# Moving the state decay, one gated C and the first state's matmul of each pair of scan chunks to earlier visits

## The chip, the core and the metric

The kernel runs on one NeuronCore of a Trainium2 chip. TensorE (PE) does matrix products into PSUM, VectorE (DVE), ScalarE (ACT) and GpSimd (POOL) work on elements, SyncE (SP) issues most of the transfers. Each engine takes its own instructions in order and waits on semaphores for the others. The metric is the device time of one execution in microseconds (us); for a version it is the median of its runs.

## The reference

One decoder layer for 1024 positions of width 1024. After a norm, one wide projection gives the inputs of two branches: a Mamba-2 scan (SSD) and forgetting attention; both are gated, merged, projected and added to x. The change touches the scan alone. Cut to that:

```python
# 16 heads of 64 channels in 4 groups that share B and C (state size 128); chunks of q = 128
da_cs = jnp.cumsum((dt * a).reshape(bsz, nc, q, g, r), axis=2)
decay = jnp.exp(jnp.where(causal[None, None, :, :, None, None], seg, -jnp.inf))
cb = jnp.einsum('bclgn,bcsgn->bclsg', cc, bc)
y_diag = jnp.einsum('bclsgr,bcsgrp->bclgrp', cb[..., None] * decay, xdt)
to_end = jnp.exp(da_cs[:, :, -1:] - da_cs)
states = jnp.einsum('bcsgn,bcsgrp->bcgrpn', bc, xdt * to_end[..., None])
chunk_decay = jnp.exp(da_cs[:, :, -1])
def step(carry, inp):
    st, dec = inp
    return carry * dec[..., None, None] + st, carry
_, prev = lax.scan(step, init, (jnp.moveaxis(states, 1, 0), jnp.moveaxis(chunk_decay, 1, 0)))
y_off = jnp.einsum('bclgn,bcgrpn->bclgrp', cc, prev) * jnp.exp(da_cs)[..., None]
y = (y_diag + y_off).reshape(bsz, seqlen, n_heads, p)
```

So a chunk's output is a part within the chunk (`y_diag`) and a part carried in by the state of the chunks before it (`y_off`), and the state goes from chunk to chunk: times the chunk's decay, plus the chunk's own contribution.

## The kernel before

All large projections run as one long stream of half products on PE (`Stream`, `Pair`; a half product is 6 matmuls of 128x128 by 128x512, a product is two of them). The weights are split into a high and a low part by ACT (line 350) and DVE (line 351) up to three products ahead into four `wop` buffers, and sums of weights come from line 356. Other work is woven in by generators: a generator does a piece of its work and yields a number n, and the stream then runs n half products (`beside`). Such a piece of work is called a visit here.

The scan is one such generator, `ssd(g)`, once for each of the four groups g of four heads. It goes over the 8 chunks in pairs (a, b = a + 1), so there are 16 pairs in the kernel. Per pair it makes these visits:

- the *turning visit*: `first(a)` and `first(b)` (line 845). PE transposes x and B and forms B^T C (tile `tr`); DVE forms `xdt` (x times dt, line 856), the masked B^T C (`cbm`, line 861) and the weighted decay matrix `m` (line 866); ACT copies the turned B (`bn`, line 864). Then `more(a)`, `more(b)` (line 881): on POOL `xe`, which is xdt times the decay to the chunk's end (line 888), on ACT the exponential of the summed decay in place in `csb` (line 894), on POOL its product with C, the gated C (line 895). The first chunk has no gated C, the last no `xe`.
- four half products, then the *output visit*: `state(a)` with the state matmul (tile `st`, one PSUM buffer), the decay multiply of the previous state on POOL (line 909) and the add on DVE (line 914; for chunk 0 a copy, line 906); `within(a)` (yps<-m,xdt), `carried(a)` (yps<-csb,new), `within(b)`, `carried(b)`, which reads the state that `state(a)` has just made; `state(b)`, whose state the next pair reads; `skipped` (line 944); and the loads of later rows of summed decays (`sums`, `csb`, three buffers).
- two half products, `decays(a + 2)` on ACT (lines 875 and 879: the decay matrix of a coming chunk), two more, `decays(b + 2)`, and the next turning visit.

The order on each engine: matmuls and everything wrapped in `pin` keep the order in which the program issues them. The rest may be set elsewhere in its engine's queue by the planner, which works with estimated times; `tc.high_priority()` puts an instruction further ahead. On POOL nearly everything in this stage is pinned, and besides the scan its queue holds the weight differences of the output projection (`weights_work`, tile `wd`, line 211), one now and then, each waiting for its own transfer.

Of the kernel before, what the change touches and what calls it, by code (L numbers as in the profile page):

```python
# [8 lines left out]
F32 = mybir.dt.float32  # L9
# [7 lines left out]
P = 128  # L17
# [4 lines left out]
NT = T // P  # L22
# [64 lines left out]
def hybrid_layer(ctx: ExitStack, tc, a, out):  # L87

    nc = tc.nc
# [37 lines left out]
    def mm(*args, **kw):  # L127
        return tc.keep_in_program_order(nc.tensor.matmul(*args, **kw))  # L128
# [679 lines left out]
    def turn_values():  # L808

        if turning and turning[0][0] + 2 <= stream.count:  # L810
            turning.pop(0)[1]()
# [22 lines left out]
    def ssd(g):  # L834
        xs, bt, ct = [groups[g][f"xs{j}"] for j in range(2)], groups[g]["bt"], groups[g]["ct"]
        hs = slice(4 * g, 4 * g + 4)
        at = [{} for _ in range(NT)]

        def sums(c):

            if c < NT:
                csb = at[c]["csb"] = sp.tile([P, 4, P], F32, tag="csb", bufs=3, name="csb")
                nc.sync.dma_start(csb, cs_dram[hs, c * P : (c + 1) * P].unsqueeze(0).to_broadcast([P, 4, P]))

        def first(c):

            cs = slice(c * P, (c + 1) * P)
            s = at[c]
            tr = pp.tile([P, HALF], F32, tag="tr", bufs=2, name="tr")
            turn(tr[:, 0:P], xs[0][:, cs])  # L850
            turn(tr[:, P : 2 * P], xs[1][:, cs])
            if c < NT - 1:
                turn(tr[:, 2 * P : 3 * P], bt[:, cs])
            mm(tr[:, 3 * P :], bt[:, cs], ct[:, cs], start=True, stop=True)
            xdt = s["xdt"] = sp.tile([P, 4, 64], F32, tag="xdt", bufs=2, name="xdt")
            nc.vector.tensor_tensor(  # L856
                xdt, tr[:, 0 : 2 * P].rearrange("p (h d) -> p h d", h=4),
                dtn[:, c, hs].unsqueeze(2).to_broadcast([P, 4, 64]), ALU.mult,
            )
            cbm = sp.tile([P, P], F32, tag="cbm", bufs=1, name="cbm")  # L860
            nc.vector.tensor_tensor(cbm, tr[:, 3 * P :], tri, ALU.mult)
            if c < NT - 1:
                bn = s["bn"] = sp.tile([P, P], F32, tag="bn", bufs=2, name="bn")
                nc.scalar.activation(bn, tr[:, 2 * P : 3 * P], AF.Copy)
            m4 = s["m4"]
            nc.vector.tensor_tensor(m4, m4, cbm.unsqueeze(1).to_broadcast([P, 4, P]), ALU.mult)

        def decays(c):

            if c < NT:  # L870
                csb = at[c]["csb"]
                m4 = at[c]["m4"] = sp.tile([P, 4, P], F32, tag="m4", bufs=2, name="m4")
                for h in range(4):
                    pin(
                        nc.scalar.activation(  # L875
                            m4[:, h, :], csb[:, h, :], AF.Relu, scale=-1.0, bias=cscol[:, c, 4 * g + h : 4 * g + h + 1]
                        )
                    )
                pin(nc.scalar.activation(m4, m4, AF.Exp, scale=-1.0))

        def more(c):

            cs = slice(c * P, (c + 1) * P)
            s = at[c]
            if c < NT - 1:
                xe = s["xe"] = sp.tile([P, 4, 64], F32, tag="xe", bufs=2, name="xe")
                pin(
                    nc.gpsimd.tensor_tensor(  # L888
                        xe, s["xdt"], tend[:, c, hs].unsqueeze(2).to_broadcast([P, 4, 64]), ALU.mult
                    )  # L890
                )
            if c > 0:
                ce = s["ce"] = s["csb"]
                pin(nc.scalar.activation(ce, ce, AF.Exp))
                pin(nc.gpsimd.tensor_tensor(ce, ce, ct[:, cs].unsqueeze(1).to_broadcast([P, 4, P]), ALU.mult))

        def state(c, prev):

            if c == NT - 1:
                return None  # L900
            s = at[c]
            st = pp.tile([P, 4, 64], F32, tag="st", bufs=1, name="st")
            mm(st, s["bn"], s["xe"], start=True, stop=True)
            new = sp.tile([P, 4, 64], F32, tag="prev", bufs=3, name="new")
            if c == 0:
                nc.vector.tensor_copy(new, st)
            else:
                pin(
                    nc.gpsimd.tensor_tensor(
                        new, prev, cdec[:, c, hs].unsqueeze(2).to_broadcast([P, 4, 64]), ALU.mult  # L910
                    )
                )
                with tc.high_priority():
                    nc.vector.tensor_tensor(new, new, st, ALU.add)
            return new

        def within(c, yps):
            s = at[c]
            cc = slice((c % 2) * P, (c % 2 + 1) * P)
            for j in range(2):  # L920
                for e in range(2):
                    h = 2 * j + e
                    mm(
                        yps[e * 64 : e * 64 + 64, j, cc], s["xdt"][:, h, :], s["m4"][:, h, :],
                        start=(c % 2 == 0 and j == 0), stop=(c == 0), skip_group_check=True,
                    )

        def carried(c, prev, yps):
            s = at[c]
            cc = slice((c % 2) * P, (c % 2 + 1) * P)  # L930
            for j in range(2):
                for e in range(2):
                    h = 2 * j + e
                    mm(
                        yps[e * 64 : e * 64 + 64, j, cc], prev[:, h, :], s["ce"][:, h, :], start=False, stop=True,
                        skip_group_check=True,
                    )

        def skipped(c, yps):

            c2 = slice((c - 1) * P, (c + 1) * P)
            for j in range(2):
                i = 2 * g + j
                nc.vector.scalar_tensor_tensor(
                    xs[j][:, c2], xs[j][:, c2], dsk[:, i : i + 1], yps[:, j, :], ALU.mult, ALU.add
                )

        prev = early = None
        for c in range(3):
            sums(c)  # L950
        yield 2
        decays(0)
        yield 2
        decays(1)
        for a in range(0, NT, 2):
            b = a + 1
            with tc.high_priority():
                first(a)
                first(b)
            if early:  # L960
                next(early, None)
            more(a)
            more(b)
            yield 2
            turn_values()
            yield 2
            yps = pp.tile([P, 2, 2 * P], F32, tag="y", bufs=1, name="yps")
            mid = state(a, prev)
            within(a, yps)
            if a:  # L970
                carried(a, prev, yps)
            within(b, yps)
            carried(b, mid, yps)
            prev = state(b, mid)
            skipped(b, yps)
            sums(a + 3)
            sums(a + 4)
            if early:
                next(early, None)
            if a == 2:  # L980

                z = sp.tile([P, T + 4], F32, tag="u", bufs=2, name="z")
                early = squares(g, 0, [z[:, half(j)] for j in range(2)])
                next(early)
            turn_values()
            yield 2
            decays(a + 2)
            turn_values()
            yield 2
            decays(b + 2)  # L990
        if g == NG - 1:
            while turning:
                turning.pop(0)[1]()
                yield 1
# [89 lines left out]
    def gated(i):  # L1084

        y, g = {}, {}

        def begin(ch):
            g[ch] = small()
            nc.sync.dma_start(g[ch], gs_dram[i, :, half(ch)])  # L1090

        begin.early = True

        def dst(ch):
            y[ch] = small()
            return y[ch]

        def post(ch):
            stream.after(1, lambda: times(y[ch], g[ch], ch))

        def times(y, g, ch):
            nc.vector.scalar_tensor_tensor(y, g, 1.0, y, ALU.add, ALU.mult)
            pin(nc.gpsimd.dma_start(ms_dram[i, :, half(ch)], y))

        return dst, post, begin
# [85 lines left out]
    ends = [final("wbs", i, gated, ops_s, nc.vector) for i in range(4)]  # L1191
# [4 lines left out]
    with tc.tile_pool(name="pro", bufs=1, reuse_waits="tile", side="right") as pro, tc.tile_pool(  # L1196
        name="prop", bufs=1, space=PSUM, reuse_waits="tile", side="right"
# [11 lines left out]
        early = ExitStack()  # L1209
# [142 lines left out]
    with tc.tile_pool(name="att", bufs=1, reuse_waits="tile", side="right") as ap, tc.tile_pool(  # L1352
# [237 lines left out]
        state, deferred = {}, []  # L1590
# [227 lines left out]
```

## Time and profile before

| | |
|---|---|
| time, median of 3 runs | 1312.7 us (1307.1 to 1314.98) |
| the profiled execution | 1316.44 us, its span 1314.7 us |
| mean granted TensorE clock | 0.986 of full speed |
| PE idle in the span | 1314.7 - 1259.9 = 54.8 us |
| scan stages | four, between about 127 and 656 us of the span |

How to read the lines that follow: in the table of busy times an engine's time stands with its share of the span. In the list of waits a line names the engine, the tile it was to write, and whom it waited for, then the total, the number of waits and the longest. A row by window gives the window, its length, the busy time of PE, PE's weight loads, DVE, ACT and POOL with the number of instructions, the granted clock, the share of the DMA engines and GB/s. A row of the timeline gives start, length, engine, line, operation and tiles (out<-in), and in brackets how long the engine had sat idle before it and who ended that. A row by tile gives the shortest, median and longest duration in ns, and the first and last start.

### The profile page before, as it was taken

The page shows a single profiled execution, that of the slowest core. Times are in us where ns is not written, and L with a number is a line of the kernel's source. Part 1 is how long each engine was busy: PE and PEld are TensorE (multiplying, and loading weights), DVE is VectorE, ACT ScalarE, POOL GpSimd, SP SyncE. Part 2 cuts the span into 40 slices and gives each one's busy share as a digit, 9 for nine tenths or more (in the row PEclk, how much of TensorE's full clock was granted, in tenths as well). Part 3 has the DMA queues.
Part 4 walks back from the last instruction along what each step waited for, and adds up shares of the span by engine and source line. Part 5 has one row for each costly group of instructions (what it writes and reads, how often), then busy time and mean ns, then how long its engine had stood idle before and what let it go on. Part 6 is the DMA issues. An engine that isn't in the chain of part 4 may idle for free.

```text
span 1314.7 us, 20757 instructions
## 1 busy us (share of the span) xinstructions
PE 1259.9 (96%) x6928; PEld 997.1 (76%) x6928; DVE 1022.4 (78%) x1993; ACT 787.4 (60%) x1719; POOL 320.4 (24%) x321
## 2 busy tenths in 40 slices
PE   6999889998999989998999999999999999999998
PEld 4688678887877878886788777777776777778886
DVE  7989866987678967897777766777689777797975
ACT  7746555556555655565554666666687666753754
POOL 3000421004310232003400223233112212347152
PEclk9999989999999989999999999999999999999999
DMA  8232533545335434454337556666688666756933
GB/s 292 79 118 69 157 106 109 179 158 184 100 118 195 136 106 145 151 164 159 120 126 257 171 193 211 218 220 202 214 268 283 230 209 217 256 177 226 365 114 103
DMA packets 152235, 233.56 MB, mean 178 GB/s; under 512 B 15200, under 2 KB 60736, under 8 KB 152128
## 3 DMA queue, kind: packets, MB, share of 16 engines
q1 hardware_dynamic: 136064, 196.08, 46.3%
q10 hardware_dynamic: 10560, 18.06, 3.6%
q0 software_dynamic: 5504, 18.09, 3.6%
q8 instruction: 54, 0.88, 0.3%
q14 instruction: 53, 0.43, 0.1%
HBM read 162.99 MB, written 72.34 MB: 179 GB/s over the span
## 4 chain that ended last, share of the span: by engine, by line
PE 40%; DVE 5%; DMA 5%; ACT 3%; issue 2%; POOL 1%; SPq 0%; DVEq 0%; ACTq 0%; POOLq 0%
PE pb L128 15%; PE pc L128 10%; PE av L128 4%; PE s L128 4%; PE pt L131 4%; PE pd L128 2%; DVE wop L351 1%; DMA xr<-in_x 1%; DMA x3l<-t_s 1%; ACT ex L1534 1%; DMA raw<-in_wbs 1%; DMA x4l<-t_w 1%; ACT wop L350 0%; DMA th<-gs_dram 0%; ACT m L875 0%
## 5 line engine op out<-in xcount | busy, mean ns | idle before, releaser
L350 ACT ACTIVATE wop<-sum 128x512 fp32r<-128x512 f32 x180 | 112.4, 627 | 126.3 <-DVE sum L356 47.0
L351 DVE TENSOR_TENSOR wop<-sum,wop 128x512 fp32r<-128x512 f32 x180 | 144.4, 803 | 48.9 <-ACT wop L350 48.0
L1534 ACT ACTIVATE ex<-ex,nm 128x512 f32<-128x512 f32 (+1 forms) x192 | 116.2, 606 | 74.8 <-DVE nm L1530 74.3
L410 ACT ACTIVATE s<-pb 128x512 f32<-128x512 f32 x143 | 84.7, 593 | 92.7 <-PE pb L128 90.7
L351 DVE TENSOR_TENSOR wop<-raw,wop 128x512 fp32r<-128x512 f32 x144 | 106.6, 741 | 33.3 <-ACT wop L350 33.1
L128 PE MATMUL pb<-x5h,wop 128*128 128x512 f32 x376 | 132.0, 409 | 0.5 <-ACT s L410 0.5
L128 PE MATMUL pb<-x0h,wop 128*128 128x512 f32 x384 | 132.3, 401 | 0.0
L128 PE MATMUL pb<-x4h,wop 128*128 128x512 f32 x384 | 130.5, 399 | 1.5 <-ACT wop L350 1.1
L128 PE MATMUL pc<-x3h,wop 128*128 128x512 f32 x384 | 130.5, 397 | 0.4 <-DVE ot L427 0.4
L128 PE MATMUL pc<-x2h,wop 128*128 128x512 f32 x384 | 129.8, 396 | 0.0
L128 PE MATMUL pb<-x6h,wop 128*128 128x512 f32 x376 | 127.4, 397 | 1.3 <-ACT s L410 1.3
L1530 DVE CUSTOM_DVE_ANT_0 ex<-s,fb 128x512 f32<-128x512 f32 (+1 forms) x192 | 96.8, 552 | 19.6 <-PE s L128 14.4
L350 ACT ACTIVATE wop<-raw 128x512 fp32r<-128x512 f32 x144 | 89.7, 624 | 34.7 <-PE pd L128 24.6
L128 PE MATMUL pd<-x1h,wop 128*128 128x512 f32 x288 | 98.3, 402 | 0.0
L128 PEld LDWEIGHTS pb<-x5h,wop 128*128 128x128 f32 x376 | 73.3, 195 | 18.1 <-issue 1.8
L128 PEld LDWEIGHTS pb<-x4h,wop 128*128 128x128 f32 x384 | 72.4, 189 | 18.5 <-ACT wop L350 1.5
L128 PEld LDWEIGHTS pb<-x0h,wop 128*128 128x128 f32 x384 | 72.9, 190 | 17.8 <-issue 2.7
L128 PEld LDWEIGHTS pc<-x3h,wop 128*128 128x128 f32 x384 | 72.4, 189 | 17.3 <-issue 1.6
L128 PEld LDWEIGHTS pb<-x6h,wop 128*128 128x128 f32 x376 | 71.0, 189 | 18.0 <-issue 1.8
L128 PEld LDWEIGHTS pc<-x2h,wop 128*128 128x128 f32 x384 | 72.1, 188 | 16.2 <-issue 1.4
L211 POOL TENSOR_TENSOR wd<-wd 128x256 f32<-128x256 f32 x32 | 30.8, 962 | 215.8 <-DMA wd<-in_wo 134.1
L888 POOL TENSOR_TENSOR xe<-xdt,tend 128x256 f32<-128x256 f32 x28 | 27.8, 994 | 211.4 <-DVE xdt L856 211.4
(313 smaller groups left out, 3046.8 us busy)
## 6 DMA issues: line engine op xcount, KB each, us to landing
raw<-in_wu SPq DMA_DIRECT2D x128, 256.0 KB
csb<-cs_dram SPq DMA_DIRECT2D x32, 256.0 KB
q<-q_dram SPq DMA_DIRECT2D x32, 256.0 KB
k<-k_dram SPq DMA_DIRECT2D x16, 512.0 KB
fb<-f_dram SPq DMA_DIRECT2D x16, 512.0 KB
rb<-st_dram SPq DMA_DIRECT2D x48, 128.0 KB
wd<-in_wo SPq DMA_DIRECT2D x40, 128.0 KB
xt<-in_x SPq DMA_DIRECT2D x8, 512.0 KB
```

Of the source, the lines that this page charges most:

```text
L128: return tc.keep_in_program_order(nc.tensor.matmul(*args, **kw))
L131: return tc.keep_in_program_order(nc.tensor.transpose(out_, in_, idn))
L211: pin(nc.gpsimd.tensor_tensor(t[out_], t[a_], t[b_], ALU.subtract))
L350: nc.scalar.activation(op[:, 0], src, AF.Copy)
L351: nc.vector.tensor_tensor(op[:, 1], src, op[:, 0], ALU.subtract)
L410: nc.scalar.activation(s, ps, AF.Copy)
L888: nc.gpsimd.tensor_tensor(xe, s["xdt"], tend[:, c, hs].unsqueeze(2).to_broadcast([P, 4, 64]), ALU.mult)
L1530: nc.vector.tensor_tensor_reduce(o, s[e][:, 0:w], fb[hp, h][:, e, 0:w], 1.0, 3.0e38, ALU.add, ALU.min, nm)
L1534: pin(nc.scalar.activation(o, o, AF.Exp, scale=-1.0, bias=nm, accum_out=hd.at(hd.sm, i, h, e)))
```

## The change

The work of `more` and `state` is cut into smaller pieces, which are set at other places between the half products. `more` becomes `ends` (the multiply that makes `xe`) and `gated` (exponential and gated C). `state` is split into `decayed` (the multiply on POOL, which makes the new tile) and `state` (the matmul and the add).

- `decayed` for chunk a comes at the end of the previous pair's output visit; for chunk b behind `state(a)`.
- `gated(a)` comes behind `decays(a)`, two half products after the previous output visit; `gated(b)` one half product behind the turning visit.
- `state(a)` comes two half products behind the turning visit, two ahead of the output visit. `state(b)` opens the output visit, where it closed it before.
- In the output visit the order is now `within(a)`, `within(b)`, `carried(a)`, `carried(b)`.
- `decays(b)` is issued one half product ahead of the turning visit. The number of half products between the visits of a pair stays eight.
- The copy of the first state has high priority, as the add has.

```diff
-        def more(c):
+        def ends(c):
             if c < NT - 1:
+                s = at[c]
                 xe = s["xe"] = sp.tile([P, 4, 64], F32, tag="xe", bufs=2, name="xe")
...
-            if c > 0:
-                ce = s["ce"] = s["csb"]
+        def gated(c):
+            if 0 < c < NT:
+                cs = slice(c * P, (c + 1) * P)
+                ce = at[c]["ce"] = at[c]["csb"]
                 pin(nc.scalar.activation(ce, ce, AF.Exp))
                 pin(nc.gpsimd.tensor_tensor(ce, ce, ct[:, cs].unsqueeze(1).to_broadcast([P, 4, P]), ALU.mult))
-        def state(c, prev):
-            if c == NT - 1:
+        def decayed(c, prev):
+            if c >= NT - 1:
                 return None
-            st = pp.tile([P, 4, 64], F32, tag="st", bufs=1, name="st")
-            mm(st, s["bn"], s["xe"], start=True, stop=True)
             new = sp.tile([P, 4, 64], F32, tag="prev", bufs=3, name="new")
-            if c == 0:
-                nc.vector.tensor_copy(new, st)
-            else:
+            if c:
                 pin(
                     nc.gpsimd.tensor_tensor(
                         new, prev, cdec[:, c, hs].unsqueeze(2).to_broadcast([P, 4, 64]), ALU.mult
                     )
                 )
-                with tc.high_priority():
+            return new
+        def state(c, new):
+            if new is None:
+                return
+            s = at[c]
+            st = pp.tile([P, 4, 64], F32, tag="st", bufs=1, name="st")
+            mm(st, s["bn"], s["xe"], start=True, stop=True)
+            with tc.high_priority():
+                if c == 0:
+                    nc.vector.tensor_copy(new, st)
+                else:
                     nc.vector.tensor_tensor(new, new, st, ALU.add)
-            return new
...
         decays(0)
-        yield 2
+        yield 1
         decays(1)
+        yield 1
+        ours = decayed(0, None)
         for a in range(0, NT, 2):
...
-            more(a)
-            more(b)
-            yield 2
+            ends(a)
+            ends(b)
             if early:
                 next(early, None)
+            yield 1
+            gated(b)
+            yield 1
+            state(a, ours)
+            theirs = decayed(b, ours)
             turn_values()
             yield 2
+            state(b, theirs)
             yps = pp.tile([P, 2, 2 * P], F32, tag="y", bufs=1, name="yps")
-            mid = state(a, prev)
             within(a, yps)
+            within(b, yps)
             if a:
                 carried(a, prev, yps)
-            within(b, yps)
-            carried(b, mid, yps)
-            prev = state(b, mid)
+            carried(b, ours, yps)
             skipped(b, yps)
+            prev, ours = theirs, decayed(a + 2, theirs)
             sums(a + 3)
             sums(a + 4)
...
             decays(a + 2)
+            gated(a + 2)
             turn_values()
-            yield 2
-            decays(b + 2)
+            yield 1
+            decays(a + 3)
+            yield 1
```

More of the change, by code (lines that the diff above doesn't have):

```diff
@@ L879, in decays @@
                 pin(nc.scalar.activation(m4, m4, AF.Exp, scale=-1.0))
-        def more(c):
-            cs = slice(c * P, (c + 1) * P)
-            s = at[c]
+        def ends(c):
             if c < NT - 1:
+                s = at[c]
                 xe = s["xe"] = sp.tile([P, 4, 64], F32, tag="xe", bufs=2, name="xe")
@@ L891, in more @@
                 )
-            if c > 0:
-                ce = s["ce"] = s["csb"]
+        def gated(c):
+            if 0 < c < NT:
+                cs = slice(c * P, (c + 1) * P)
+                ce = at[c]["ce"] = at[c]["csb"]
                 pin(nc.scalar.activation(ce, ce, AF.Exp))
                 pin(nc.gpsimd.tensor_tensor(ce, ce, ct[:, cs].unsqueeze(1).to_broadcast([P, 4, P]), ALU.mult))
-        def state(c, prev):
-            if c == NT - 1:
-                return None
-            s = at[c]
-            st = pp.tile([P, 4, 64], F32, tag="st", bufs=1, name="st")
-            mm(st, s["bn"], s["xe"], start=True, stop=True)
+        def decayed(c, prev):
+            if c >= NT - 1:
+                return None
             new = sp.tile([P, 4, 64], F32, tag="prev", bufs=3, name="new")
-            if c == 0:
-                nc.vector.tensor_copy(new, st)
-            else:
+            if c:
                 pin(
@@ L946, in skipped @@
                 )
-        prev = early = None
+        early = prev = None
         for c in range(3):
```

## The prediction, made before the changed kernel ran

> **What bounds the kernel now.** I read the page first (busy times, 40 slices), then who waits for whom on PE, then busy times by stage, then the timeline of single visits. One execution: 1316.4 us, span 1314.7 us.
>
> ```profile
> span 1314.7 us, 20757 instructions
> ...
> PE 1259.9 (96%) x6928; PEld 997.1 (76%) x6928; DVE 1022.4 (78%) x1993; ACT 787.4 (60%) x1719; POOL 320.4 (24%) x321
> ...
> PEclk9999989999999989999999999999999999999999
> ```
>
> PE is busy for 96% of the span, so time can only come from its 55 us of idle or from its clock, which is below full in two slices. The idle is concentrated. Waits of PE between 90 and 700 us (in total, times, longest):
>
> ```profile
> PE yps L128 <- DVE new L914: 19.6, 10, 3.8
> PE yps L128 <- POOL csb L895: 5.0, 7, 2.0
> ```
>
> So 24.6 us are lost at one place, the matmuls of `carried` (yps<-csb,new): mostly for the new state, a little for the gated C. By stage (length, PE, PEld, DVE, ACT, POOL busy, clock); the first four rows are the four scan stages, the last a stretch between two of them:
>
> ```profile
> 127.00:204.00 77.00, 67.36 (x383) 54.58 (x382) 58.99 (x98) 42.15 (x97) 26.07 (x24) 0.93 0.40 125
> 296.00:368.00 72.00, 66.78 (x404) 54.13 (x403) 55.43 (x95) 41.95 (x97) 27.49 (x23) 0.98 0.44 139
> 443.00:512.00 69.00, 64.31 (x385) 52.05 (x384) 53.21 (x91) 39.68 (x92) 26.16 (x24) 0.95 0.42 136
> 512.00:585.00 73.00, 73.00 (x328) 60.47 (x327) 62.77 (x101) 42.09 (x73) 4.30 (x5) 1.00 0.48 157
> 585.00:656.00 71.00, 65.30 (x386) 52.73 (x385) 54.60 (x92) 40.56 (x95) 26.56 (x23) 0.95 0.43 134
> ```
>
> The scan stages are 289 us long with 263.75 us of PE. Their clock is 0.93, 0.98, 0.95, 0.95, full elsewhere beside them: 0.07 x 77 + 0.02 x 72 + 0.05 x 69 + 0.05 x 71 = 13.8 us of lost clock. Stalls and lost clock together are 38.4 us, the most that this change can win. From 512 to 585 us PE never idles: 73.00 / 328 = 0.223 us a matmul, so a half product (6) is 1.34 us.
>
> One visit shows the chain (second pair of the first group). POOL's rows, all it did there (start, length):
>
> ```profile
> 150.32 0.62 POOL L888 TENSOR_TENSOR xe<-xdt,tend 128x256 f32<-128x256 f32 x1 [5.81 <-DVE xdt L856]
> 155.46 1.45 POOL L895 TENSOR_TENSOR csb<-csb,ct 128x512 f32<-128x512 f32 x1 [4.52 <-ACT csb L894]
> 156.87 1.06 POOL L888 TENSOR_TENSOR xe<-xdt,tend 128x256 f32<-128x256 f32 x1
> 157.90 1.71 POOL L895 TENSOR_TENSOR csb<-csb,ct 128x512 f32<-128x512 f32 x1
> 159.56 1.17 POOL L211 TENSOR_TENSOR wd<-wd 128x256 f32<-128x256 f32 x1
> 160.69 0.61 POOL L909 TENSOR_TENSOR new<-new,cdec 128x256 f32<-128x256 f32 x1
> ```
>
> The same visit on ACT, DVE and PE (start, length):
>
> ```profile
> 150.80 0.26 ACT L864 ACTIVATE bn<-tr 128x128 f32<-128x128 f32 x1
> ...
> 154.59 0.27 ACT L864 ACTIVATE bn<-tr 128x128 f32<-128x128 f32 x1
> ...
> 155.70 1.76 DVE L866 TENSOR_TENSOR m<-m,cbm 128x512 f32<-128x512 f32 x1
> ...
> 161.33 0.42 DVE L914 TENSOR_TENSOR new<-new,st 128x256 f32<-128x256 f32 x1 [1.19 <-POOL new L909]
> ...
> 149.90 0.39 PE L128 MATMUL tr<-ct,bt 128*128 128x128 f32 x2
> ...
> 155.59 0.59 PE L128 MATMUL st<-xe,bn 128*128 128x256 f32 x2
> ...
> 161.81 0.66 PE L128 MATMUL yps<-csb,new 128*64 128x128 f32 x8 [3.64 <-DVE new L914]
> ```
>
> st(a) was through at 156.18. The decay multiply (L909) came only at 160.69, since POOL works in issue order: behind both gated C, the second end product and a weight difference. Its add ended at 161.75, PE went on at 161.81. The DVE add that PE "waits for" is 0.42 us of this; POOL's queue is the rest.
>
> **The change part by part.** It adds and removes no arithmetic: 24 decay multiplies, 28 gated C, 28 end products, 28 state matmuls stay. It moves no DMA. What moves, on which queue:
>
> ```profile
> L895 POOL TENSOR_TENSOR csb<-csb,ct x28: 1296/1704/1832, 140.8 to 649.5; 128x512 f32<-128x512 f32 x28
> ...
> L909 POOL TENSOR_TENSOR new<-new,cdec x24: 607/1026/1064, 143.5 to 651.2; 128x256 f32<-128x256 f32 x24
> L914 DVE TENSOR_TENSOR new<-new,st x24: 403/414/422, 144.7 to 653.3; 128x256 f32<-128x256 f32 x24
> ...
> L866 DVE TENSOR_TENSOR m<-m,cbm x32: 674/744/1783, 137.0 to 648.7; 128x512 f32<-128x512 f32 x32
> ```
>
> *Decay multiply.* a's moves to the end of the previous output visit, eight half products (10.7 us) ahead; b's to behind state(a), two halves (2.7 us) ahead of its add. Both need at most 1.06 us. On POOL, a's waits for the previous state's add, and behind it stand a weight difference and the next gated C, due two halves later: nothing. *state(a)* goes two halves behind the transposes, its add two halves ahead of the output visit: 2.7 us against 0.42 plus queue. carried(b) then finds its state ready. I take 19.6 us of waits to 0. st(a) itself needs xe(a) and bn(a), ready at 150.94 and 151.06 in the visit above, against 150.2 + 2.7 = 152.9: nothing, with 1.8 us to spare. The one `st` bank is free again by then.
>
> *Gated C.* a's exponential and 1.70 us multiply go ahead of the turning visit, so POOL has xe(b) next after xe(a). b's is issued one half later than before, but without a's in front. The 5.0 us go for a; for b they can stay in the first pair of a group, which has no a to move (below).
>
> *decays(b)* is issued one half earlier (three instead of four behind the output visit); its csb row was asked for at the end of that visit, and no ACT wait on that transfer shows in the views, so nothing.
>
> *What is late next.* st(b) moves from the tail of the output visit to its head, and within(b) comes right behind within(a). Ordinary visits: bn(b) was ready at 154.86, st(b) is due at 155.59, fine; but m(b) ended at 157.46 and within(b) is due at 155.59 + 0.52 + 0.44 = 156.55. That is 0.9 us at worst; at best the half earlier decays cover it. That multiply was 1.76 us instead of 0.74 while POOL ran beside it, so I lean to the low end: 0.2 us x 12 visits = 2.2 us. First visits of a group:
>
> ```profile
> 589.06 0.39 PE L128 MATMUL tr<-ct,bt 128*128 128x128 f32 x2
> ...
> 594.77 0.59 PE L128 MATMUL st<-xe,bn 128*128 128x256 f32 x2
> ...
> 596.19 0.66 PE L128 MATMUL yps<-m,xdt 128*64 128x128 f32 x8 [0.24 <-DVE m L866]
> 597.32 0.66 PE L128 MATMUL yps<-csb,new 128*64 128x128 f32 x8 [0.47 <-POOL csb L895]
> ```
>
> Here 0.24 + 0.47 us stood already; the half earlier decays (1.34 us) can remove both, or both stay and bn(b) adds some 0.4. Between 0 and 1.1 us x 4, I take 0.4 x 4 = 1.5 us. New waits: 3.7 us (0 to 15.2).
>
> *DVE.* Without stalls and lost clock the first stage would last 62.0 us (67.36 - 5.4) with 58.99 us of DVE, 95%; the other three come to 85, 87 and 88%. The densest stretch above that feeds PE without idle has 62.77 / 73 = 86%. At that share the first stage needs 68.6 us, 6.6 more; at best nothing, since weights are split several products ahead. I take 2 us.
>
> *Clock.* Stalls drag the clock down behind them (rows by window, clock in the third column from the end; then PE's timeline):
>
> ```profile
> 163.00:166.00 3.00, 3.00 (x9) 2.39 (x8) 2.37 (x4) 0.86 (x2) 0.74 (x1) 0.54 0.33 78
> 166.00:169.00 3.00, 3.00 (x15) 2.48 (x14) 1.61 (x3) 1.69 (x4) 0.00 (x0) 1.00 0.12 19
> 637.50:640.90 3.40, 3.40 (x11) 2.68 (x10) 0.00 (x0) 0.25 (x1) 0.00 (x0) 0.60 0.78 241
> ```
> ```profile
> 634.45 0.66 PE L128 MATMUL yps<-csb,new 128*64 128x128 f32 x8 [0.87 <-DVE new L914]
> 635.03 0.70 PE L128 MATMUL st<-xe,bn 128*128 128x256 f32 x2
> 635.57 0.95 PE L128 MATMUL pv<-ones,z 128*128 128x1 f32 x8
> ```
>
> After the 3.64 us stall three microseconds held 9 matmuls instead of 15 (1.3 us lost). But at 637.5 the clock fell too, behind a stall of only 0.87 us among small matmuls, so short gaps may still do it. I leave one such drop (1.4 us) and take back 12.4 of 13.8 us (bounds 0 and 13.8).
>
> The Trainium skill, "TensorE: Matmul & The Clock Gate", Part 1, says that PE goes to half rate only after an idle window of about 3.4 us. By that rule none stays and the sum is 1.4 us better; the row at 637.5 speaks against it.
>
> Sum: -19.6 - 5.0 + 3.7 + 2.0 - 12.4 = -31.3 us. On the profiled 1316.4 us that is 1285.1. That execution stands 3.7 us above the median of the three runs (1312.7), so I predict 1281 us.
>
> **The rivals.**
>
> *Waits under other names.* m(b), the gated C of b or bn(b) are late at most visits (at its worst 15.2 us as above), and drops of the clock follow. With half the waits and half the lost clock left: 24.6/2 + 13.8/2 = 19.2 us, 1293. For it: ACT issues bn(b) and the exponentials late in the visits above. Against: all that they hang on (decays, xe(b), the other gated C) is issued earlier than before.
>
> *Nothing left in the way.* No new waits, no lost clock: -38.4, 1274. This is where the skill's rule on the clock would end.
>
> *DVE becomes the bound through POOL.*
>
> ```profile
> 158.20:161.80 3.60, 0.00 (x0) 0.00 (x0) 2.34 (x3) 0.00 (x0) 3.10 (x3) 1.00 0.36 78
> ```
>
> In that stall POOL was busy for 3.10 of 3.60 us, at no cost to PE. Moved, this work runs beside DVE; L866 shows 1.78 against 0.67 us. If 0.86 x 24.6 = 21 us were added to DVE in full, its 222.2 us in the four stages become 243; at 86% that is 283 us instead of 289: -6, 1307. Against: DVE keeps 28 us idle in the shortened stages, and POOL beside it is in the 222.2 in part already.
>
> The skill's "SBUF — State Buffer" calls that port pair an exclusive lock between the two, which is what this case needs; the 1.78 us agrees.
>
> *Slower.* st(a) now stands among the half products, and PE works in order: if xe(a) is late, projections stop too. POOL has a wait that could do it:
>
> ```profile
> POOL wd L211 <- DMA wd<-in_wo: 134.1, 14, 19.1
> ```
>
> A weight difference queued ahead of xe(a) whose transfer hasn't landed holds POOL for 9.6 us on average. The gain of 31 us is spent after some three to four such cases in front of an xe(a), and 1% slower comes at five. Against: they arise between the visits, POOL idle otherwise; in the visit above POOL had been idle for 5.81 us when xdt released xe(a).
>
> **How the numbers follow.** 1% of 1312.7 is 13.1 us, about what a measurement can tell from no change: faster below 1299.6, slower above 1325.8. Chances: forecast 0.56, waits under other names 0.20 (a tenth of it within 1%), nothing left 0.12, DVE bound 0.08 (within 1%), slower 0.04. So faster 0.56 + 0.18 + 0.12 = 0.86, same 0.10, slower 0.04. The range: 1274 less 4 us of spread between runs below; above, most of the second case, 1300. It leaves out DVE, slower and some tails, 0.15 to 0.2.
>
> **What would show it.** Right: yps<-DVE new gone from PE's waits, csb under 2 us; the clock in the four stages at 0.99 or more; L909 long done when its add starts; xe(b) right behind xdt(b); the scan stages together 31 us shorter, everything behind 656 us shifted unchanged. Wrong: PE waits at st for xe or bn, at yps<-m for L866, or a DVE share over 90% with PE waiting for wop; or the same clock drops without stalls.

## The result, and the profile after

The changed kernel takes 1305.39 us (median of 22 runs, 1301.62 to 1309.67), the kernel before 1311.58 us (22 runs). The ratio is 0.9958, 95% interval 0.9947 to 0.9969: 6 us faster, clear of noise and a fifth of the 31 us that were forecast. That is above the stated range (1270 to 1300) and, by the prediction's own 1%, the case "same", to which it gave 0.10. The profiled execution spans 1303.1 us, against 1314.7.

The page of the changed kernel, same lines as before:

```profile
span 1303.1 us, 20775 instructions
...
PE 1250.7 (96%) x6928; PEld 990.0 (76%) x6928; DVE 1021.4 (78%) x1993; ACT 787.9 (60%) x1719; POOL 315.6 (24%) x321
...
PEclk9999989999999999999999999999999999999999
```

Idle PE is still 1303.1 - 1250.7 = 52.4 us, where it was 54.8; busy PE fell by 9.2 us although it has the same 6928 matmuls. So the waits did not go, and the same matmuls took less time: that is the clock, with one 8 among the slices where there were two. The waits of PE between 90 and 690 us (total, times, longest):

```profile
PE st L128 <- POOL xe L887: 20.8, 12, 4.4
PE st L128 <- ACT bn L864: 2.4, 2, 1.3
PE st L128 <- DVE new L924: 1.4, 1, 1.4
PE yps L128 <- DVE m L866: 1.4, 1, 1.4
PE tr L131 <- ACT th L826: 0.6, 1, 0.6
PE tr L131 <- DVE xs L795: 0.5, 1, 0.5
PE pb L128 <- DVE wop L351: 0.3, 1, 0.3
```

Both old waits of `carried` are gone to the last tenth: 24.6 us, as forecast. In their place the state matmul waits for `xe`, 20.8 us, a wait that the kernel before did not have. With the others the list comes to 27.4 us, against 26.5 before.

The longest, 4.40 us, is in the third pair. POOL's rows, all that it did there (start, length, idle before and who ended it), then one row each of DVE, ACT and PE:

```profile
161.24 0.96 POOL L907 TENSOR_TENSOR new<-new,cdec 128x256 f32<-128x256 f32 x1 [1.29 <-PE yps L128]
172.02 1.27 POOL L898 TENSOR_TENSOR csb<-csb,ct 128x512 f32<-128x512 f32 x1 [9.82 <-ACT csb L897]
173.25 1.17 POOL L211 TENSOR_TENSOR wd<-wd 128x256 f32<-128x256 f32 x1
174.38 2.08 POOL L887 TENSOR_TENSOR xe<-xdt,tend 128x256 f32<-128x256 f32 x2
...
167.84 0.42 DVE L856 TENSOR_TENSOR xdt<-tr,dtn 128x256 f32<-128x256 f32 x1 [0.56 <-PE tr L128]
...
171.33 0.62 ACT L897 ACTIVATE csb<-csb 128x512 f32<-128x512 f32 x1
...
175.49 1.22 PE L128 MATMUL st<-xe,bn 128*128 128x256 f32 x2 [4.40 <-POOL xe L887]
```

`xdt` of a was there at 168.26 and POOL had been idle since 162.20. But the head of POOL's queue was now the gated C of a, which waited for its exponential on ACT until 171.95; then came a weight difference, and only then `xe`, 6 us late. PE, which works in order, stood at the state matmul, and the projections behind it stood too. It is so at eleven of the twelve visits: the gated C of a stands ahead of `xe` on POOL, at five of them with a weight difference between the two, and these five have the four longest waits among them. (At the twelfth, a wait of 0.70 us, `xe` followed `xdt` at once.)

### The profile page after: what moved, and what is told of

Read it like the earlier page. It is cut to its first block, busy times and chain, and to the rows that moved or that the text cites. A ratio compares the mean times of both kernels' runs of the same rounds, so it can differ in the third digit from the quotient of the medians.

```text
span 1303.1 us, 20775 instructions
## 1 busy us (share of the span) xinstructions
PE 1250.7 (96%) x6928; PEld 990.0 (76%) x6928; DVE 1021.4 (78%) x1993; ACT 787.9 (60%) x1719; POOL 315.6 (24%) x321
## 4 chain that ended last, share of the span: by engine, by line
PE 70%; DVE 9%; issue 7%; DMA 6%; ACT 4%; POOL 3%; SPq 0%; DVEq 0%; ACTq 0%; POOLq 0%
PE pb L128 28%; PE pc L128 18%; PE pd L128 5%; PE pt L131 5%; PE av L128 4%; PE s L128 4%; DMA raw<-in_wu 2%; PE yps L128 2%; DVE wop L351 2%; PE st L128 1%; DVE sum L356 1%; ACT ex L1551 1%; DMA xt<-in_x 1%; POOL xe L887 1%; POOL csb L898 1%
## 5 line engine op out<-in xcount | busy, mean ns | idle before, releaser
L351 DVE TENSOR_TENSOR wop<-sum,wop 128x512 fp32r<-128x512 f32 x180 | 141.7, 788 | 50.4 <-ACT wop L350 49.2
L351 DVE TENSOR_TENSOR wop<-raw,wop 128x512 fp32r<-128x512 f32 x144 | 111.2, 773 | 32.9 <-ACT wop L350 32.8
L128 PEld LDWEIGHTS pb<-x0h,wop 128*128 128x128 f32 x384 | 73.1, 190 | 17.9 <-issue 2.7
L356 DVE TENSOR_TENSOR sum<-raw 128x512 f32<-128x512 f32 x68 | 51.5, 757 | 32.6 <-DMA raw<-in_wu 29.5
```

The lines of the kernel that those rows point to most:

```text
L351: nc.vector.tensor_tensor(op[:, 1], src, op[:, 0], ALU.subtract)
L356: self.adds.tensor_tensor(t, x, y, ALU.add)
```

## The experiments

Two theories. A: `xe(a)` is late since the change put the gated C of a ahead of it on POOL, an engine that works in order. B: the first state matmul is too early for what ACT delivers, whatever POOL does. First, the suspected blocker moved and nothing else, the exponential left where the change put it:

```diff
                 pin(nc.scalar.activation(ce, ce, AF.Exp))
-                pin(nc.gpsimd.tensor_tensor(ce, ce, ct[:, cs].unsqueeze(1).to_broadcast([P, 4, P]), ALU.mult))
+
+        def times_c(c):
+            if 0 < c < NT:
+                cs = slice(c * P, (c + 1) * P)
+                ce = at[c]["ce"]
+                pin(nc.gpsimd.tensor_tensor(ce, ce, ct[:, cs].unsqueeze(1).to_broadcast([P, 4, P]), ALU.mult))
...
             ends(a)
             ends(b)
+            times_c(a)
...
             gated(b)
+            times_c(b)
             yield 1
```

> The changed kernel with one thing moved: the POOL multiply that makes the gated C of chunk a is issued behind both end products (xe) of the turning visit, not ahead of them; its exponential on ACT stays early. Theory A (POOL's order: xe(a) stands behind the gated C of a, which waits for its exponential): PE's wait at st for xe falls from 20.8 us to under 4 us, no wait at yps for csb above 2 us, at most one drop of the clock in the scan stages, time about 1280 us (1274 to 1290). Theory B (the state matmul of a is too early for what ACT delivers, whatever POOL does): the waits at st stay at 12 us or more under the name of bn or of the add, time 1297 or more.

Measured: 1287.01 us, ratio 0.9833 (0.9789 to 0.9877). The longest of PE's waits:

```profile
PE st L128 <- ACT bn L864: 8.8, 9, 3.1
PE st L128 <- POOL xe L887: 2.5, 1, 2.5
PE yps L128 <- DVE m L866: 1.3, 1, 1.3
PE st L128 <- DVE new L930: 1.2, 1, 1.2
```

and POOL in the third pair:

```profile
165.59 0.73 POOL L211 TENSOR_TENSOR wd<-wd 128x256 f32<-128x256 f32 x1 [4.11 <-DMA wd<-in_wo]
167.47 1.19 POOL L887 TENSOR_TENSOR xe<-xdt,tend 128x256 f32<-128x256 f32 x2 [1.15 <-DVE xdt L856]
171.15 2.99 POOL L904 TENSOR_TENSOR csb<-csb,ct 128x512 f32<-128x512 f32 x2 [2.49 <-ACT csb L897]
```

Both end products now follow `xdt` at once, and the gated C waits for ACT behind them. The weight difference, which stood between the two before, now runs while POOL has nothing else. The wait for `xe` fell from 20.8 to 2.5 us; the one that is left, at 189 us, comes from an `xdt` that was late on DVE. Theory A holds. A part of B does too: the waits for `bn` rose from 2.4 to 8.8 us, and all waits at `st` come to 13.6 us, over the 12 that B named, but the time is 10 us under B's. Next, the whole gated C of a late, exponential and all:

```diff
             ends(a)
             ends(b)
+            gated(a)
...
             decays(a + 2)
-            gated(a + 2)
```

> The changed kernel with the whole gated C of chunk a (exponential and multiply) issued in the turning visit behind the end products, as it was before the change; decay multiply and state matmul stay early. Theory A: as good as with the multiply alone moved, st waits under 4 us, time 1275 to 1292; the early exponential has no worth of its own. Theory B: st waits of 12 us or more, 1297 or more. If the early exponential is worth something, waits at yps for csb come back (5 us) and the time is 5 us above the run with the multiply alone moved.

Measured: 1287.58 us, ratio 0.982 (0.9796 to 0.9844). Waits at `st` for bn 5.7, at `yps` for csb 2.9 us. All waits at `st` come to 7.5 us, not to under 4. So moving the exponential ahead gains nothing that shows: it goes with 2.9 us less of csb and 3.1 us more of bn. Most of the latter, 2.6 us, is one visit (332 us), where ACT sat idle for 2.29 us until a transfer of csb had landed, ahead of the exponentials and `bn`. These two are the fastest versions found, about 24 us below the kernel before. Then the other side of the same conflict: POOL's order as changed, but the state matmul put back.

```diff
-            state(a, ours)
-            theirs = decayed(b, ours)
             turn_values()
             yield 2
-            state(b, theirs)
             yps = pp.tile([P, 2, 2 * P], F32, tag="y", bufs=1, name="yps")
+            state(a, ours)
+            theirs = decayed(b, ours)
             within(a, yps)
-            within(b, yps)
             if a:
                 carried(a, prev, yps)
+            within(b, yps)
             carried(b, ours, yps)
+            state(b, theirs)
             skipped(b, yps)
```

> The changed kernel with the state matmul of a, and the decay multiply of b behind it, put back to the head of the output visit and the old order within it; POOL's order is that of the changed kernel. Theory A: no wait at st for xe (over 2 us in total), since the state matmul comes two half products later; what stays is carried(b) waiting for the add behind some 1.4 us of other matmuls, 3 to 8 us in total; time 1280 to 1293. Theory B says the same of the waits at st. If the early state matmul was worth its place, carried(b) waits 12 us or more and the time is 1297 or more.

Measured: 1292.56 us, ratio 0.9864 (0.9834 to 0.9895). The wait for `xe` is 2.2 us, one time. `carried(b)` waits 5.7 us for the new state (4.7 for the add, 1.0 for the copy of a group's first state), `yps` 4.9 us for m. So the early place of the state matmuls, with the order that goes with it, may be worth some 5 us where POOL's order lets it (the intervals touch), and costs about 13 us where it doesn't. And the decay multiply alone, on the kernel before:

```diff
         decays(1)
+        ours = decayed(0, None)
...
-            mid = state(a, prev)
+            state(a, ours)
+            theirs = decayed(b, ours)
...
-            carried(b, mid, yps)
-            prev = state(b, mid)
+            carried(b, ours, yps)
+            state(b, theirs)
             skipped(b, yps)
+            prev, ours = theirs, decayed(a + 2, theirs)
```

(`decayed` and `state` cut as in the change.)

> The kernel before with one part of the change alone: the decay multiply of a at the end of the previous output visit, that of b behind the first state matmul; all else as before. If the decay multiply's place in POOL's queue was the cause of the 19.6 us, yps waits for the new state fall under 6 us, those for csb stay about 5 us, time 1283 to 1297. If the add was late for another cause (DVE's own queue), the waits stay over 14 us and the time is that of before, 1306 to 1314.

Measured: 1292.71 us, ratio 0.9864 (0.9839 to 0.9888).

```profile
PE yps L128 <- POOL csb L895: 11.9, 11, 2.0
PE yps L128 <- DVE new L921: 3.8, 7, 1.1
```

The place of the decay multiply in POOL's queue was the cause of the old wait: 19.6 us became 3.8. What was behind it shows up, the gated C with 11.9 us for the 5.0 expected. One part of the change alone gains three times what the whole gains.

The gain of the change itself needs a cause, as its waits are no smaller. Theory C: fewer drops of the clock. Both kernels were profiled once more.

> The changed kernel as it is, profiled a second time. Theory C (the change's own gain is no wait that went, but fewer drops of the clock behind the waits): waits of PE in the scan stages again 24 to 28 us, st for xe again about 21 us; drops of the clock to one half 10 to 20 us in the scan stages, fewer than in the kernel before. If the number of drops is chance from run to run, it may be anything from 3 to 30 us, and the time follows it by half.

> The kernel before as it is, profiled a second time. Theory C: waits of PE for the new state and the gated C again about 25 us, half clock again 24 to 34 us before 660 us, more than in the changed kernel by 10 us or more. If the drops are chance, the difference to the changed kernel is gone.

Measured: changed 26.3 us of waits and 13.7 us at half clock; before 26.2 and 27.3 (the first profiles: 27.4 and 13.7; 26.5 and 30.7 in this part of the kernel). Two profiles of each are few, but every run lists its granted clock. In the 22 runs of the changed kernel it is 0.992 to 0.996, and the clock lost, (1 - clock) x span, is 8.3 us in the mean; in the 31 runs of the kernel before that were taken beside the experiments it is 0.985 to 0.992, and 14.9 us. The difference of 6.6 us is the whole gain: span less lost clock is 1294.6 us before and 1295.6 us after. So theory C holds. What makes the drops fewer when the waits are not comes in the last section.

Next, a dose: the first state matmul of the changed kernel one half product later.

```diff
             gated(b)
             yield 1
-            state(a, ours)
-            theirs = decayed(b, ours)
             turn_values()
-            yield 2
+            yield 1
+            state(a, ours)
+            theirs = decayed(b, ours)
+            yield 1
```

> The changed kernel with the first state matmul (and b's decay multiply behind it) one half product later, three behind the turning visit: 1.34 us more for xe to arrive, POOL's order the same. Theory A: the twelve waits at st for xe (0.56 to 4.40 us, 20.8 us in all) each shrink by 1.34 us or to nothing: 20.8 - 13.3 = 7.5 us stay, the two waits for bn are unchanged (they are b's), time 1285 to 1295. Theory B: the waits at st stay at 15 us or more.

Measured: 1298.25 us, ratio 0.9891 (0.9863 to 0.9918).

```profile
PE st L128 <- DVE new L924: 6.2, 5, 2.8
PE st L128 <- POOL xe L887: 6.2, 5, 3.1
PE st L128 <- DVE new L922: 3.5, 2, 2.0
```

The wait for `xe` is 6.2 us where 7.5 were worked out, so the dose acts as theory A says. The time missed its range, since 9.7 us now stand at `st` for the new state, where 1.4 stood: there is one `st` bank, and the second state matmul now follows the first by one half product, too soon for the first add (or copy) to have read it. A version meant to be better:

```diff
             ends(b)
+            gated(a)
...
+            turn_values()
+            yield 1
             state(a, ours)
             theirs = decayed(b, ours)
-            turn_values()
-            yield 2
-            state(b, theirs)
+            yield 1
...
             carried(b, ours, yps)
+            state(b, theirs)
             skipped(b, yps)
...
-            gated(a + 2)
```

> What the runs so far suggest as the better version: gated C of a behind the end products, first state matmul three half products behind the turning visit, second state matmul at the end of the output visit again. Waits at st for bn (5.7 us with the gated C late alone) go, those for csb stay about 3 us, some waits at yps for m may come (0 to 4 us): together 4 to 8 us instead of 12; time 1281 to 1287, no more than one drop of the clock in the scan stages. If it isn't faster than the version with the gated C late, those waits for bn came back under other names.

Measured: 1293.51 us, ratio 0.985 (0.9818 to 0.9881), a miss: bn is gone from the waits at `st`, but `yps` waits 6.7 us for csb and 6.1 us for m, and the clock dropped twice, not once. A likely reason is that with the second state matmul gone from the head of the visit the matmuls that need m and csb come sooner; as three things were moved at once, that is not shown.

Last, the waits for `bn`. In the version with the gated C late one visit shows a reason on ACT:

```profile
136.44 0.62 ACT L350 ACTIVATE wop<-sum 128x512 fp32r<-128x512 f32 x1
139.89 0.28 ACT L864 ACTIVATE bn<-tr 128x128 f32<-128x128 f32 x1 [2.83 <-DVE cbm L861]
```

ACT sat idle until DVE was through with `cbm` of the same chunk, which reads the same PSUM tile and is issued ahead of `bn`. The two exchanged, on both good versions:

```diff
-            cbm = sp.tile([P, P], F32, tag="cbm", bufs=1, name="cbm")
-            nc.vector.tensor_tensor(cbm, tr[:, 3 * P :], tri, ALU.mult)
             if c < NT - 1:
                 bn = s["bn"] = sp.tile([P, P], F32, tag="bn", bufs=2, name="bn")
                 nc.scalar.activation(bn, tr[:, 2 * P : 3 * P], AF.Copy)
+            cbm = sp.tile([P, P], F32, tag="cbm", bufs=1, name="cbm")
+            nc.vector.tensor_tensor(cbm, tr[:, 3 * P :], tri, ALU.mult)
```

> The version with the whole gated C of a late, and in the turning visit the copy of the turned B (bn, ACT) issued ahead of the masked product (cbm, DVE) of the same chunk. In the run without this ACT sat idle for 2.83 us until cbm of b was through, although bn doesn't read it. Theory D (bn waits for cbm only since it is issued behind it on the same PSUM tile): the waits of PE at st for bn fall from 5.7 us to under 2 us, time 1281 to 1286. If the waits stay at 4 us or more, cbm isn't what holds bn. If the waits go and the time stays at 1287, they came back as waits for m or csb.

> The version with only the multiply of the gated C of a behind the end products, with the same exchange of bn and cbm. Theory D: waits at st for bn fall from 8.8 us to under 3 us, time 1279 to 1285. If bn was late because ACT is taken up by the early exponentials, the waits stay at 5 us or more and the time at 1287.

Measured: 1296.55 us, ratio 0.9903 (0.9883 to 0.9923), and 1307.0 us, ratio 0.9962 (0.9947 to 0.9976). The first one's waits:

```profile
PE yps L128 <- DVE m L866: 8.2, 8, 2.5
PE tr_v L131 <- DVE cbm L864: 5.8, 4, 1.6
PE st L128 <- POOL xe L887: 2.1, 1, 2.1
PE st L128 <- DVE new L924: 1.5, 1, 1.5
PE st L128 <- ACT bn L862: 1.4, 1, 1.4
```

bn fell from 5.7 to 1.4 us (8.8 to 2.5 in the other), as theory D says. But now `cbm`, and so m, is late, and `tr_v` waits for the PSUM tile that `cbm` holds: 14.0 us (22.1 in the other) for the 4 to 6 won. So theory D is right on the cause of the waits for bn, and both times missed their ranges. Two buffers for `cbm` weren't tried.

All twelve profiled executions fit one sum. The table gives the waits of PE between 90 and 690 us, the time at half clock ahead of the kernel's end, and the span less the waits and less half of the half clock time:

| version | waits | half clock | span | rest |
|---|---|---|---|---|
| before, first and second profile | 26.5; 26.2 | 34.1; 27.3 | 1314.7; 1309.1 | 1271.1; 1269.2 |
| changed, first and second profile | 27.4; 26.3 | 13.7; 13.7 | 1303.1; 1300.1 | 1268.9; 1267.0 |
| multiply of the gated C behind xe | 15.2 | 3.4 | 1285.7 | 1268.8 |
| whole gated C late | 12.7 | 3.4 | 1287.1 | 1272.7 |
| state matmul put back | 16.5 | 10.2 | 1291.1 | 1269.5 |
| decay multiply alone | 17.9 | 10.2 | 1293.8 | 1270.8 |
| state matmul half a product later | 20.9 | 13.7 | 1298.4 | 1270.7 |
| gated C late, state matmuls later | 16.1 | 6.8 | 1291.3 | 1271.8 |
| the two with bn ahead | 21.0; 28.1 | 3.4; 17.1 | 1294.2; 1308.0 | 1271.5; 1271.4 |

The rest lies between 1267 and 1273 us while the spans differ by 29. So these two terms account for the differences to within 6 us. The sum is bookkeeping and shows where the time went, not why. From before to changed (first profiles) the waits rose by 0.9 us and half the half clock fell by 10.2 us, of 11.6 us of span; with the second profiles it is 6.8 of 9.0 us.

## Why the prediction was wrong, point by point

**Where the time is lost** (24.6 us at `carried`, the chain through POOL's queue): right. The decay multiply alone took the wait for the new state from 19.6 to 3.8 us.

**Decay multiply, 19.6 us to 0; gated C, 5.0 us to 0**: right as sizes, both waits are 0 in the changed kernel.

**"st(a) itself needs xe(a) and bn(a), ... nothing, with 1.8 us to spare"**: this step failed. The margin was read from the order of before, in which POOL had nothing ahead of `xe(a)`. The next paragraph, on the gated C, put one there and said only that `xe(b)` gains. Taken together the two would have shown it: a multiply of 1.30 us or more, whose own input comes from a busy ACT, in front of an operation that has 1.8 us. Put at nothing, the wait measured 20.8 us, at twelve of sixteen visits; with that multiply moved behind `xe` it measured 2.5 us. The prediction did list "PE waits at st for xe" among the signs that it is wrong.

**The rival "slower"** named the right place and mechanism, `xe(a)` late on POOL and the projections stopped with it, but the weight differences as blocker. In the visit shown one of them took 1.17 us of the 6, and one stood there at five of the twelve visits; the gated C and its exponential are the rest. Its chance of 0.04 was for a loss; that the same mechanism could just eat the gain was not among the cases.

**The rival "waits under other names"** (1293 us, 0.20) had the outcome in kind. It expected m(b), the gated C of b or bn(b) late and half the waits left. What came was `xe(a)`, and the waits came back whole.

**New waits, 3.7 us (0 to 15.2)**: bn 2.4, the add 1.4 and m 1.4 come to 5.2 us, within the bounds. The wait at `st` for the add's bank, said to be none, is the 1.4 us.

**DVE, 2.0 us, and the rival that DVE becomes the bound**: not seen. Waits for wop are 0.3 us in the changed kernel, and in the two shortest versions the rest in the table is 1268.8 and 1272.7 us: one within the others' range, the other 1 us above it, so a term of that size can't be excluded. That this rival's 1307 us lie nearest to the measured time is luck.

**Clock, 12.4 us back**: right in kind, too large, and for another reason than forecast. In the four stages the changed kernel got 6.8 us back, (27.3 - 13.7) / 2, with waits as large as before; the version with the multiply moved got 12.0 us back, (27.3 - 3.4) / 2. (Of the 30.7 us above, one drop of 3.4 us, at 418 us, lies between two stages.) The forecast leaned on the waits being gone. They were not, and the drops became fewer, most likely since the single waits became shorter (last section). That a stall of 0.87 us among small matmuls is enough for a drop, which the prediction read from one row, held in one of the two profiles.

So the sum with measured terms is -24.6 + 26.0 (xe and the new waits) - 6.8 = -5.4 us, near the 6.2 us between the medians of 22 runs each. The two profiled executions lie 11.6 us apart; 3.4 us of that is what two drops of the clock cost outside the four stages, at 418 and 1149 us, which only the first profile before has. With the failed step mended the kernel took 1287 us where 1281 were forecast; its waits for bn, 8.8 us, are as large as what is missing.

## What to carry to other kernels

A slack that was read from a trace holds only for the queue order of that trace: when several things move, write out each engine's new order, and ask of each operation what stands ahead of it and what that one waits for. On an engine that works in order an operation that is issued early but whose input comes late is a plug; issue it behind the one that is urgent, even if it is ready later. And count a long stall twice, once as idle time and once as the clock behind it.

## What the runs showed of the hardware that was not expected

The same total of waits cost different amounts of clock: 26.5 and 26.2 us of waits brought 30.7 and 27.3 us at half clock in this part of the kernel before, 27.4 and 26.3 us brought 13.7 in the changed one. Each drop lasts 3.41 us or twice that (the last one, at the kernel's end, apart). In the first profile of the changed kernel they stand behind the waits of 4.40, 2.88 and 2.25 us:

```profile
174.50:181.30 6.80, 5.81 (x14) 4.65 (x15) 4.85 (x6) 0.78 (x2) 4.37 (x4) 0.53 0.31 116
321.30:324.80 3.50, 3.50 (x12) 2.74 (x11) 0.42 (x2) 0.60 (x1) 1.81 (x2) 0.57 0.57 173
642.20:645.60 3.40, 3.40 (x10) 2.66 (x9) 2.26 (x3) 0.00 (x0) 1.05 (x1) 0.57 0.56 188
```

The drops of one execution begin whole multiples of 3.413 us apart, to within 0.01 us, in all twelve executions, the one at the kernel's end included. So the clock is set on a grid of steps that runs through the whole execution, and it matters how a wait lies on it. The same wait of the same kernel brought a drop in one profile and none in the other:

| wait of PE | first profile | second profile |
|---|---|---|
| before, `yps` for the new state | 0.87 us, to 634.45: drop | 0.88 us, to 633.03: none |
| changed, `st` for xe | 2.12 us, to 500.02: none; PE 52% busy in its step | 2.15 us, to 499.82: drop; PE 37% busy in its step |
| changed, `st` for xe | 2.25 us, to 641.62: drop; PE 34% busy in its step | 1.95 us, to 641.53: none; parted over two steps, 72% and 71% |

Counted over all twelve profiled executions, from 100 to 1250 us: PE was busy for less than 46% of the time in 32 of 4044 steps, and each of the 32 was followed by a step at half clock. Of the other 4012 steps 14 were. Eight of these were at half clock themselves; five held mostly small matmuls, as at the 0.87 us wait, so small ones may count for less; in the last, ahead of 418 us, two waits of 1.09 and 0.41 us stood between full products. The 46% are read off these traces afterwards, with PE's busy time as the profile models it, and no run varied it.

That gives a reason for the change's own gain. The waits add up to the same, but five of 2.6 us or more stand in each profile of the kernel before and two in each of the changed one, and a drop stood at every one of these. A long wait mostly empties a step, a short one mostly doesn't. Length alone does not decide: 3.08 us (to 332.29, multiply of the gated C behind xe) lay across two steps that stayed 59% and 51% busy, and brought no drop.

The Trainium skill, "TensorE: Matmul & The Clock Gate", Part 1, gives 3.4 us both as the idle window that brings half rate and as the step in which the clock is set. The length of the drops agrees; that a whole window must be idle does not, as only one of the 32 steps was wholly idle.
